# Both transposing transfers of a pair at one place, the last head's first group by TensorE, the last group half a product later

## The chip, the cores and the metric

The kernel runs on one core of one Trainium2 chip. The metric is the device time of one execution in microseconds (us), less is better; several runs are told by their median. Engines are named as the profile names them: PE is TensorE (matmul; PEld its weight loads), DVE is VectorE, ACT is ScalarE, POOL is GpSimd, SP is SyncE. SP computes nothing here; it issues transfers, one after the other, and a transfer whose data aren't ready holds up those behind it in SP's order. POOL issues a few transfers of its own.

## The reference

A decoder trunk of two layers on x of 1 x 1024 x 1024 in float32. Layer 0 is dilated attention: 8 heads of width 128, each in three groups (window, dilation) = (128, 1), (512, 4), (2048, 16); rotary positions on q and k; the three groups of a head are merged by their softmax denominators. Layer 1 is a gated linear attention. After each mixer stands a squared-ReLU MLP; each sub-layer is normalized ahead and added to x. What the change touches is layer 0's attention up to its output product:

```python
qkv = (h @ w_in).reshape(B, S, N_GROUPS, 3, ATTN_HEADS, HEAD_DIM)
for g, (window, dil) in enumerate(DILATED_GROUPS):
    q = apply_rope(qkv[:, :, g, 0], cos, sin) * (HEAD_DIM ** -0.5)
    k = apply_rope(qkv[:, :, g, 1], cos, sin)
    v = qkv[:, :, g, 2].astype(jnp.float32)
    o_g, lse_g = dilated_group_attention(q, k, v, dil, window // dil)
    outs.append(o_g); lses.append(lse_g)
alpha = jax.nn.softmax(jnp.stack(lses, axis=0), axis=0)
o = jnp.sum(alpha[..., None] * jnp.stack(outs, axis=0), axis=0)
return o.reshape(B, S, ATTN_WIDTH).astype(h.dtype) @ w_out
```

## The kernel before, in words

float32 products are made of three matmuls of split operands (`...h` is the high part, `...l` the low one). The attention of layer 0 runs as 24 rounds p = 3 h + g, one for each head h and group g. `Heads.run_head` gives a round 14 half products of 12 matmuls or fewer, in the slots 0, 1, 3, 2, 6, 4, 5; they make q and k of round p (banks `pX`, `pY`, `pV`, `pZ`). `advance()` after each half product moves a clock by one step, and whatever is entered in the agenda for that step (`at(step, function, rank)`) is written into the program there, by rank. So the order of every engine is fixed by the numbers in those calls; with c = 14 p, "c + 3" is the third step of round p.

Of round p itself come: copies of banks by ACT (`e`, L1166), `column` (DVE adds `c`, L1129; SP swaps its halves by two transfers into `cw`, L1130 and L1131; a few steps later DVE multiplies with the rotary tables, L1138 and L1139, and adds into `qT` or `kT`, L1141 or L1146), the loading of raw weights for the next round (`load`, L1121) and their splitting by ACT and DVE (L536, L537).

Entwined with round p, `follow(p - 1, ...)` does the attention of the round before, in four pairs j of query blocks: `scores` (PE, `pS`, L989), `soft` (DVE and ACT, L1003 and L1005, into `pt`), a transposition of `pt`, and `values` (PE, `pO`, L1069; then ACT copies `orow`, L1073, and SP stores it to `og`, L1076 to L1082). The transposition has two forms. `turn` lets PE transpose (`pP`, L1016), and ACT copies the result (L1018). For groups 0 and 2 it goes by memory instead: `halves` (ACT separates the 16-bit halves, L1035; POOL writes them to `pscr`, L1037) and `flip` (SP reads them back by a transposing transfer, `pt<-pscr`, L1048). Pair 0 of group 0 has two such transfers, since its blocks have unequal numbers of keys. `POINTS` holds the steps for scores, turn, values and flip of the four pairs, counted from the round in which the attention is followed; steps of 14 and more fall in the round after it. Attention of group 0 is followed in rounds with p mod 3 = 1, and its flips fall in p mod 3 = 2; those of group 2 fall in p mod 3 = 1.

In rounds p mod 3 = 1 the merge of the head before is entered (`plan_merges`): SP loads `rows` (L1209) in the round p mod 3 = 2, DVE makes minima, differences and shares (`mz`, `md`, `me`, L1216 to L1225), ACT scales by them (L1229), DVE adds (`om`, L1233).

In the last round (p=23) four raw pieces of the output weights (`W.dma`, L136) and the first half of the merged heads 0 to 3 (`ol`, `ahead_h8`, L1294) are loaded, and PE transposes `ol` (`pT`, L260). `tail` then follows the last group beside the output product (`pd`, L214 to L216).

Of the kernel before, what the change touches and what calls it, by code (L numbers as in the profile page):

```python
# [20 lines left out]
P = 128  # L21
# [4 lines left out]
HEADS = 8  # L26
# [16 lines left out]
def hybrid_trunk(ctx, tc, x, norm_mix, norm_mlp, norm_fin, a_in, a_out, g_in, g_up, g_b, g_nw,  # L43
                 g_out, m_up, m_down, tab, msk, gmask, ident_d, out):
    nc = tc.nc
    pe, act, dve, pool, sp = nc.tensor, nc.scalar, nc.vector, nc.gpsimd, nc.sync
# [7 lines left out]
    def h8(shape, dt, name):  # L54
        return wk.tile(shape, dt, name=name, tag="h8", bufs=12)

    def k4(shape, dt, name):
        return wk.tile(shape, dt, name=name, tag="k4", bufs=25)

    def t2(shape, dt, name):  # L60
        return wk.tile(shape, dt, name=name, tag="t2", bufs=8)
# [50 lines left out]
    class Weights:  # L112
# [14 lines left out]
            self.slots.append(src)  # L127
            self.by.append(by)

        def dma(self, by=None):  # L130
            n = self.ndma
            if n < len(self.slots):
                self.ndma += 1
                src = self.slots[n]
                self.raws[n] = k4([P] + list(src.shape[1:]), F32, "raw")
                (by or sp).dma_start(self.raws[n], src)  # L136

        def prep(self, eng=dve):
            n = self.nprep
# [41 lines left out]
    W = Weights()  # L181
# [8 lines left out]
    def add_rows(w, k0, by=None):  # L190
        for k in range(2):
            W.add(w[P * (k0 + k):P * (k0 + k + 1), :], by and by(k0 + k))
# [93 lines left out]
    class Split:  # L286
# [4 lines left out]
        @staticmethod  # L291
        def at(tiles, k):
            n = 4 // len(tiles)
            return tiles[k // n][:, k % n, :]
# [442 lines left out]
    oscr = drp.tile([S, D], F32, name="oscr")  # L737
# [209 lines left out]
    def advance():  # L947
        clock[0] += 1
        for _, fn in sorted(agenda.pop(clock[0], []), key=lambda e: e[0]):
            fn()  # L950
# [9 lines left out]
    def load_values(g, h):  # L960

        v = k4([P, NB, HD], F32, "v")
        c = slice(HD * h, HD * h + HD)
        if g == 0:
            sp.dma_start(v, vscr.rearrange("(b p) g c -> p b g c", p=P)[:, :, 0, c])
        elif g == 1:
            for b in range(2):
                sp.dma_start(v.rearrange("p (r b) c -> p r b c", b=2)[:, :, b, :],
                             vscr[512 * b:512 * b + 512].rearrange("(p r) g c -> p r g c", r=4)[:, :, 1, c])
        else:  # L970
            sp.dma_start(v, vscr.rearrange("(p r) g c -> p r g c", r=8)[:, :, 2, c])
        return v
# [6 lines left out]
    class Attention:  # L979
# [102 lines left out]
                    sp.dma_start(to.rearrange("(p r) c -> p r c", r=8)[:, 2 * j - 2:2 * j + 2, :], row)  # L1082

        def plan(self, c, points, turn, values, flip=None):
            self.by_dma = flip is not None and self.g in (0, 2)
            if flip is not None and not self.by_dma:
                turn, values = (12, 12, 16, 16), (16, 16, 18, 18)

            def get():
                self.v = load_values(self.g, self.h)  # L1090
            at(c + points[0] - 2, get)
            for j in range(4):
                t = c + points[j]
                at(t, lambda j=j: self.scores(j), 2)
                at(t + 1 + (j % 2 and points[j] == points[j - 1]), lambda j=j: self.soft(j), 2)
                if self.by_dma:
                    at(c + turn[j], lambda j=j: self.halves(j), 3)
                    at(c + flip[j], lambda j=j: self.flip(j), 3)
                else:
                    at(c + turn[j], lambda j=j: self.turn(j), 3)  # L1100
                at(c + values[j], lambda j=j: self.values(j), 4)

    class Heads(Up):
# [54 lines left out]
        def plan(self, p):  # L1158
            c = 14 * p
            st = self.st.setdefault(p, {})  # L1160
            self.behind = True

            def keep(b, name):
                def fn():
                    e = t2([P, 512], F32, name)
                    act.activation(e, st[b], AF.Copy)  # L1166
                    st[name] = e
                return fn
            at(c + 3, keep("X", "e1"), 0)
            at(c + 5, lambda: self.column(p, 0, 0, st["Y"], st["e1"]), 1)  # L1170
            at(c + 7, keep("V", "e5"), 0)
            at(c + 9, keep("X", "e2"), 0)
            at(c + 11, lambda: self.column(p, 1, 0, st["V"], st["e2"]), 1)
            at(c + 13, keep("X", "e3"), 0)
            at(c + 13, lambda: self.column(p, 1, 1, st["X"], st["e5"]), 1)
            at(c + 15, lambda: self.column(p, 0, 1, st["Z"], st["e3"]), 1)
            if p == 0:
                for s, t in ((4, 1), (6, 3), (5, 5)):
                    at(c + t, lambda s=s: self.stage(p, s), 7)
            at(c + 1, lambda: self.load(p + 1))  # L1180
            for s, t in ((0, 8), (1, 9), (2, 10), (3, 11), (4, 14), (6, 15), (5, 17)):
                at(c + t, lambda s=s: self.stage(p + 1, s), 7)

        def run_head(self, p):
            self.plan(p)
            if p:
                self.follow(p - 1, 14 * p, self.POINTS if p < self.count - 1 else self.SINGLE)
            for s in self.SLOTS:
# [1 line left out]
                    self.product(p, s, range(2 * half, 2 * half + 2))  # L1190
                    advance()

        POINTS = (8, 8, 12, 12), (11, 12, 15, 16), (21, 21, 25, 25), (14, 15, 18, 19)
        SINGLE = (8, 10, 12, 14), (12, 14, 16, 18), (14, 16, 18, 20)

        def follow(self, p, c, points):
# [91 lines left out]
                reached.add((0, half))  # L1288
            at(clock[0] + 7, last)

    def ahead_h8(pairs, by=sp):

        t = h8([P, 4, 512], F32, "ol")
        by.dma_start(t, oscr[512 * pairs:512 * pairs + 512, 0:512].rearrange("(b p) c -> p b c", p=P))  # L1294
        return [t[:, 0:2, :], t[:, 2:4, :]]

    def ahead_k4(p):
# [4 lines left out]
    def plan_merges(h, c):  # L1302

        rows, part = {}, {}

        def load(half):
            rows[half] = merge_load(h, half)

        def weigh(half):
            part[half] = merge_weights(rows[half])  # L1310

        def join(half):
            del part[half]
            merged(h, half, merge_join(rows.pop(half), dve))
        for half in range(2):
            t = c + 14 + 11 * half
            at(t, lambda half=half: load(half))
            if half and h == HEADS - 2:
                t += 8
            at(t + 4, lambda half=half: weigh(half), 9)  # L1320
            at(t + 5, lambda half=half: merge_shares(rows[half], *part[half]), 9)
            for n in range(4):
                at(t + 6 + n, lambda half=half, n=n: merge_scale(rows[half], part[half][1], n), 9)
            at(t + 10, lambda half=half: join(half), 9)
# [383 lines left out]
    for i, n in enumerate(plan[:-5]):  # L1708
# [5 lines left out]
        if n == vals.STEPS - 2:  # L1714
            heads = Heads(vals.h)
# [38 lines left out]
    ol = []  # L1754
    turned = Turned(ol, x[0])
    for p in range(heads.count):
        h, g = divmod(p, NG)
        if g == 1 and h:
            plan_merges(h - 1, 14 * p)
        if p == heads.count - 1:  # L1760
            for k in range(0, KT, 2):
                add_rows(a_out, k)
            c = 14 * p
            at(c + 1, lambda: (W.dma(pool), W.dma(pool)), 0)
            at(c + 2, lambda: (W.dma(pool), W.dma(pool)), 0)
            at(c + 3, lambda: ol.extend(ahead_h8(0, pool)), 0)
            for t in (5, 6, 7, 8):
                at(c + t, lambda: W.prep(dve), 7)
            at(c + 8, lambda: turned.turn(0), 7)
            at(c + 9, lambda: (turned.load_x(0), turned.load_x(1)))  # L1770
            at(c + 11, lambda: turned.turn(1), 7)
            at(c + 17, lambda: ol.extend(ahead_h8(1)), 9)
        heads.run_head(p)
# [7 lines left out]
    def tail():  # L1781

        c = clock[0]
        heads.follow(heads.count - 1, c, ((6, 7, 8, 9), (9, 10, 11, 12), (11, 12, 13, 14)))
        load, start, finish = merges(HEADS - 1, merged)
        rows = {}
        advance()

        def early(half):
            t = rows[half] = h8([P, 4, 512], F32, "ol2")  # L1790
            sp.dma_start(t[:, :, 0:384], oscr[512 * half:512 * half + 512, 512:896].rearrange("(b p) c -> p b c", p=P))
        at(c + 7, lambda: early(0))
        at(c + 16, lambda: early(1))
        for i, (half, h) in enumerate(((0, 4), (0, 5), (0, 6), (1, 4), (1, 5), (1, 6))):
            at(c + (13 + 3 * i if half == 0 else 21 + i), lambda half=half, h=h: t_head(h, half, rows[half][:, :, HD * (h - 4):HD * (h - 4) + HD]))
        at(c + 15, lambda: (load(0), load(1)), 9)
        at(c + 18, lambda: start(0))
        at(c + 19, lambda: finish(0))
        at(c + 20, lambda: start(1))
        at(c + 21, lambda: finish(1))  # L1800
        steps.extend([advance] * 42)

    tail()


# [587 lines left out]
    ol, turn1 = [], []  # L2393
# [81 lines left out]
```

## Time and profile before

| what | value |
|---|---|
| median of three runs | 2601.3 us (2597.0, 2601.3, 2602.2) |
| profiled execution | 2598.51 us |
| its span, first to last instruction | 2596.7 us |
| mean granted clock of TensorE | 0.998 |
| PE busy | 2574.3 us (99%) |
| DVE, ACT, POOL busy | 72%, 50%, 2% |
| stage of the 24 rounds | from about 246 to 855 us of the span |

The page gives busy times by engine, groups of instructions and transfers. The answers of the trace quoted below are of three kinds: timelines (start, length, engine, line, operation, what it writes and reads, count; in brackets the idle time of the engine ahead of it and what ended it), waits (who waited for what: total, times, longest) and windows (for each engine the busy time in a stretch and the number of instructions, then the granted clock, the busy share of the DMA engines and GB/s).

### The profile page before, as it was taken

The page shows a single profiled execution, that of the slowest core. Times are in us where ns is not written, and L with a number is a line of the kernel's source. Part 1 is how long each engine was busy: PE and PEld are TensorE (multiplying, and loading weights), DVE is VectorE, ACT ScalarE, POOL GpSimd, SP SyncE. Part 2 cuts the span into 40 slices and gives each one's busy share as a digit, 9 for nine tenths or more (in the row PEclk, how much of TensorE's full clock was granted, in tenths as well). Part 3 has the DMA queues.
Part 4 walks back from the last instruction along what each step waited for, and adds up shares of the span by engine and source line. Part 5 has one row for each costly group of instructions (what it writes and reads, how often), then busy time and mean ns, then how long its engine had stood idle before and what let it go on. Part 6 is the DMA issues. An engine that isn't in the chain of part 4 may idle for free.

```text
span 2596.7 us, 33212 instructions
## 1 busy us (share of the span) xinstructions
PE 2574.3 (99%) x11985; PEld 2142.2 (82%) x11985; DVE 1864.0 (72%) x3018; ACT 1298.7 (50%) x2360; POOL 51.8 (2%) x81
## 2 busy tenths in 40 slices
PE   9999999999998999999999999999999999999998
PEld 7888888888887888888888888888888888888887
DVE  7745888888887768666657587887657866656567
ACT  6423455656655446555534345654326554553334
POOL 0000000000001000000000000000000000000000
PEclk9999999999999999999999999999999999999999
DMA  5543677777778633554775452463513544396543
GB/s 183 170 141 115 153 179 200 176 201 196 196 205 221 208 122 127 170 168 139 278 260 182 140 195 96 133 200 98 195 65 118 170 157 155 130 356 203 183 149 131
DMA packets 377911, 445.70 MB, mean 172 GB/s; under 512 B 68145, under 2 KB 240561, under 8 KB 377746
## 3 DMA queue, kind: packets, MB, share of 16 engines
q1 hardware_dynamic: 372850, 428.63, 53.5%
q0 software_dynamic: 4752, 14.68, 1.7%
q8 instruction: 94, 1.54, 0.2%
q14 instruction: 71, 0.58, 0.1%
q10 hardware_dynamic: 144, 0.26, 0.0%
HBM read 279.19 MB, written 127.60 MB: 157 GB/s over the span
## 4 chain that ended last, share of the span: by engine, by line
PE 65%; DVE 3%; ACT 1%; DMA 1%; issue 1%; SPq 0%; DVEq 0%; ACTq 0%
PE pB L1938 13%; PE pX L599 10%; PE pA L1938 10%; PE pV L599 7%; PE pY L599 3%; PE pZ L599 3%; PE pd L216 3%; PE pd L214 3%; PE pd L215 3%; PE pB L830 3%; PE pA L830 2%; PE pT L335 1%; DMA cw<-c 1%; PE pO L2236 1%; PE pU L2218 0%
## 5 line engine op out<-in xcount | busy, mean ns | idle before, releaser
L1938 PE MATMUL pB<-dh 128*128 128x512 f32 x512 | 199.4, 389 | 0.0
L1938 PE MATMUL pB<-dh,dl 128*128 128x512 f32 x512 | 199.2, 389 | 0.0
L1938 PE MATMUL pB<-dl,dh 128*128 128x512 f32 x512 | 199.2, 389 | 0.0
L223 DVE TENSOR_TENSOR dl<-sin,dh 128x1024 fp32r<-128x1024 f32 x112 | 136.8, 1221 | 42.4 <-ACT dh L220 41.8
L220 ACT ACTIVATE dh<-sin 128x1024 fp32r<-128x1024 f32 x112 | 117.8, 1052 | 88.4 <-PE pB L1938 33.4
L220 ACT ACTIVATE dh<-kept 128x1024 fp32r<-128x1024 f32 x64 | 67.9, 1061 | 183.3 <-DVE kept L1903 138.1
L599 PE MATMUL pV<-s4h,wd 128*128 128x512 f32 x448 | 150.3, 397 | 0.0
L1938 PE MATMUL pA<-dl,dh 128*128 128x512 f32 x384 | 149.4, 389 | 0.0
L1938 PE MATMUL pA<-dh,dl 128*128 128x512 f32 x384 | 149.4, 389 | 0.0
L1938 PE MATMUL pA<-dh 128*128 128x512 f32 x384 | 149.4, 389 | 0.0
L1005 ACT ACTIVATE pt<-pt,orow 128x128 f32<-128x128 f32 (+1 forms) x192 | 84.7, 443 | 75.7 <-DVE orow L1003 74.4
L1938 PEld LDWEIGHTS pB<-dh 128*128 128x128 f32 x512 | 96.2, 188 | 19.9
L1938 PEld LDWEIGHTS pB<-dl,dh 128*128 128x128 f32 x512 | 96.2, 188 | 19.9
L1938 PEld LDWEIGHTS pB<-dh,dl 128*128 128x128 f32 x512 | 96.1, 188 | 19.8
L537 DVE TENSOR_TENSOR wal<-raw,wah 128x512 fp32r<-128x512 f32 x112 | 76.2, 687 | 40.8 <-ACT wah L536 40.8
L537 DVE TENSOR_TENSOR wbl<-t,wbh 128x1024 fp32r<-128x1024 f32 x56 | 68.6, 1225 | 43.9 <-ACT wbh L536 43.8
L599 PEld LDWEIGHTS pV<-s4h,wd 128*128 128x128 f32 x448 | 84.2, 188 | 19.3 <-ACT e L1166 1.7
L608 ACT ACTIVATE c<-c 128x512 f32<-128x512 f32 x64 | 40.4, 631 | 118.6 <-DVE c L636 77.5
L223 DVE TENSOR_TENSOR dl<-kept,dh 128x1024 fp32r<-128x1024 f32 x64 | 78.4, 1225 | 24.7 <-ACT dh L220 18.7
L599 PE MATMUL pX<-s3h,wgh 128*128 128x512 f32 x224 | 89.3, 399 | 2.4 <-ACT e L1166 2.4
L599 PE MATMUL pZ<-a22h,wgh 128*128 128x512 f32 x224 | 90.1, 402 | 0.0
L599 PE MATMUL pX<-s2h,wbh 128*128 128x512 f32 x224 | 89.0, 397 | 0.0
(400 smaller groups left out, 7378.7 us busy)
## 6 DMA issues: line engine op xcount, KB each, us to landing
sin<-acts SPq DMA_DIRECT2D x112, 512.0 KB, 3.9
raw<-in_mlp_w_up_dram SPq DMA_DIRECT2D x64, 512.0 KB, 6.0
acts<-s SPq DMA_DIRECT2D x64, 512.0 KB, 3.5
raw<-in_mlp_w_down_dram SPq DMA_DIRECT2D x64, 512.0 KB, 4.8
raw<-in_attn_w_in_dram SPq DMA_DIRECT2D x98, 256.0 KB, 4.7
cw<-c SPq DMA_DIRECT2D x192, 128.0 KB, 2.8
acts<-c SPq DMA_DIRECT2D x64, 256.0 KB, 2.2
kept<-in_mlp_w_down_dram SPq DMA_DIRECT2D x32, 512.0 KB, 5.8
```

Of the source, the lines that this page charges most:

```text
L214: pe.matmul(ps, sh, mh, start=start, stop=False)
L215: pe.matmul(ps, sh, ml, start=False, stop=False)
L216: pe.matmul(ps, sl, mh, start=False, stop=stop)
L220: act.activation(hi, src, AF.Copy)
L223: dve.tensor_tensor(lo, src, hi.bitcast(F32), op=OP.subtract)
L335: pe.transpose(ps[:, k, 128 * i:128 * i + 128], xn[i][:, c:c + 128], ident)
L537: self.remain(lambda: dve.tensor_tensor(lo, src, hi.bitcast(F32), op=OP.subtract))
L599: pe.matmul(st[b], u[:, k, :], v, start=first and k + n == 0, stop=k == 3 and n == 2, skip_group_check=True)
L608: act.activation(r, r, AF.Relu)
L830: pe.matmul(self.acc[s][t], a[:, c], b[:, k, :], start=fresh and m + k + v == 0, stop=m == 1 and k == 1 and v == 2, skip_group_check=True)
L1005: act.activation(pt[:, i, :128 * n], pt[:, i, :128 * n], AF.Exp, scale=-1.0, bias=m, accum_out=self.row[:, r, HD:HD + 1])
L1938: pe.matmul(self.acc[s][t], a[:, k, c], b[:, k, :], start=fresh and m + k + v == 0, stop=m == 7 and k == 1 and v == 2, skip_group_check=True)
```

## The change

Five things, all in layer 0's attention:

1. `plan`: the last head (h = 7) doesn't transpose group 0 by memory any more; PE does, at the steps that group 1 has. Its group 2 was done by PE already.
2. The raw output weights and the first `ol` of the last round are issued by SP, not by POOL, at the same steps.
3. Raw weights of the next round are loaded at c + 3, not c + 1.
4. The flips stand at steps 14, 14, 18, 18, not 14, 15, 18, 19.
5. In the tail, all steps of the last group are one later.

```diff
-        def dma(self, by=None):
+        def dma(self):
...
-                (by or sp).dma_start(self.raws[n], src)
+                sp.dma_start(self.raws[n], src)
...
         def plan(self, c, points, turn, values, flip=None):
-            self.by_dma = flip is not None and self.g in (0, 2)
+            self.by_dma = flip is not None and self.g in (0, 2) and self.h < HEADS - 1
             if flip is not None and not self.by_dma:
                 turn, values = (12, 12, 16, 16), (16, 16, 18, 18)
...
-            at(c + 1, lambda: self.load(p + 1))
+            at(c + 3, lambda: self.load(p + 1))
...
-        POINTS = (8, 8, 12, 12), (11, 12, 15, 16), (21, 21, 25, 25), (14, 15, 18, 19)
+        POINTS = (8, 8, 12, 12), (11, 12, 15, 16), (21, 21, 25, 25), (14, 14, 18, 18)
...
-    def ahead_h8(pairs, by=sp):
+    def ahead_h8(pairs):
...
-        by.dma_start(t, oscr[512 * pairs:512 * pairs + 512, 0:512].rearrange("(b p) c -> p b c", p=P))
+        sp.dma_start(t, oscr[512 * pairs:512 * pairs + 512, 0:512].rearrange("(b p) c -> p b c", p=P))
...
-            at(c + 1, lambda: (W.dma(pool), W.dma(pool)), 0)
-            at(c + 2, lambda: (W.dma(pool), W.dma(pool)), 0)
-            at(c + 3, lambda: ol.extend(ahead_h8(0, pool)), 0)
+            at(c + 1, lambda: (W.dma(), W.dma()), 0)
+            at(c + 2, lambda: (W.dma(), W.dma()), 0)
+            at(c + 3, lambda: ol.extend(ahead_h8(0)), 0)
...
-        heads.follow(heads.count - 1, c, ((6, 7, 8, 9), (9, 10, 11, 12), (11, 12, 13, 14)))
+        heads.follow(heads.count - 1, c, ((7, 8, 9, 10), (10, 11, 12, 13), (12, 13, 14, 15)))
```

SP's order in the rounds p mod 3 = 2 (here p=5), `-` before and `+` now:

```order
+L1048 DMA_TRANSPOSE pt<-pscr_93 128x2x512
 L1209 DMA rows<-og_70 128x4x390
 L1130 DMA cw<-c 64x512
 L1131 DMA cw<-c 64x512
-L1048 DMA_TRANSPOSE pt<-pscr_93 128x2x512
 L1121 DMA raw<-in_attn_w_in_dram 128x4x128 x4
 L1048 DMA_TRANSPOSE pt<-pscr_94 128x2x512
-L1130 DMA cw<-c 64x512
-L1131 DMA cw<-c 64x512
 L1048 DMA_TRANSPOSE pt<-pscr_95 128x2x512
+L1130 DMA cw<-c 64x512
+L1131 DMA cw<-c 64x512
```

The second pair's transfer now stands ahead of the merge's `rows` and of a pair of `cw`, and the fourth pair's ahead of the next pair of `cw`; the raw weights keep their place behind the first `cw`.

SP's order in the last round (p=23), before:

```order
L1048 DMA_TRANSPOSE pt<-pscr_92 128x1x256
L1048 DMA_TRANSPOSE pt<-pscr_92 128x2x256
L1209 DMA rows<-og_76 128x4x390
L1130 DMA cw<-c 64x512
L1131 DMA cw<-c 64x512
L1048 DMA_TRANSPOSE pt<-pscr_93 128x2x512
L1048 DMA_TRANSPOSE pt<-pscr_94 128x2x512
L1130 DMA cw<-c 64x512
L1131 DMA cw<-c 64x512
L1048 DMA_TRANSPOSE pt<-pscr_95 128x2x512
L968 DMA v<-vscr 128x4x128 x2
```

and now:

```order
L1209 DMA rows<-og_76 128x4x390
L136 DMA raw<-in_attn_w_out_dram 128x1024 x2
L1130 DMA cw<-c 64x512
L1131 DMA cw<-c 64x512
L136 DMA raw<-in_attn_w_out_dram 128x1024 x2
L1076 DMA og_77<-orow 128x4x130
L1294 DMA ol<-oscr 128x4x512
L1076 DMA og_77<-orow 128x4x130
L1130 DMA cw<-c 64x512
L1131 DMA cw<-c 64x512
L968 DMA v<-vscr 128x4x128 x2
```

The five transposing transfers are gone; weights and `ol` stand among the small ones, and the stores `og` of group 0, which followed `v` before, come ahead of the second `cw`.

PE's order in the tail, at the first scores of the last group, `-` before and `+` now:

```order
 L215 MATMUL pd<-wlo,oTh 128x512
 L216 MATMUL pd<-whi,oTl 128x512
-L989 MATMUL pS<-kT,qT 128x128 x2
 L1069 MATMUL pO<-v,pt 128x128 x3
 L989 MATMUL pS<-kT,qT 128x128 x2
```

The first scores of the last group stand behind the last `pO` of the group before; the second scores move behind the twelve matmuls that follow.

## The prediction

> **What bounds the kernel now.** I read the page first, then the waits of TensorE over the stage that the change touches, then the timelines of the places where those waits sit.
>
> ```profile
> PE 2574.3 (99%) x11985; PEld 2142.2 (82%) x11985; DVE 1864.0 (72%) x3018; ACT 1298.7 (50%) x2360; POOL 51.8 (2%) x81
> ```
>
> TensorE (PE) is busy for 99% of the span, so an edit can gain only what is left of its idle time, or time lost at a lower clock. The list of waits from 246 to 866 us (the 24 rounds of layer 0's attention and the start of its tail) shows how little that is. Columns: total us, times, longest.
>
> ```profile
> PE pO L1069 <- DMA pt<-pscr: 7.0, 5, 5.4
> PE pX L599 <- ACT e L1166: 2.4, 7, 1.1
> PE pS L989 <- DVE qT L1146: 2.2, 3, 1.7
> ...
> PEld pV L599 <- ACT e L1166: 1.7, 6, 0.4
> ```
>
> Five waits for a transposing transfer (`pt<-pscr`) make 7.0 us, one of them alone 5.4. That one stands in the last round (p=23):
>
> ```profile
> 826.17 0.39 PE L599 MATMUL pX<-s2h,wbl 128*128 128x512 f32 x1
> 826.40 0.83 PE L1069 MATMUL pO<-v,pt 128*128 128x128 f32 x6
> 832.63 2.07 PE L1069 MATMUL pO<-v,pt 128*128 128x128 f32 x8 [5.41 <-DMA pt<-pscr]
> ...
> 835.36 0.63 PE L599 MATMUL pX<-s2h,wbl 128*128 128x512 f32 x1
> 835.79 0.63 PE L599 MATMUL pX<-s2h,wbh 128*128 128x512 f32 x1
> ...
> 837.07 0.82 PE L989 MATMUL pS<-kT,qT 128*128 128x128 f32 x4
> 837.72 1.04 PE L260 MATMUL pT<-ident,ol 128*128 128x128 f32 x8
> ```
>
> After the wait the matmuls start 0.43 us apart (835.36 to 835.79) instead of 0.23 (826.17 to 826.40): a half clock, until 837.07. From 832.63 to 837.07 that costs half of 4.44, **2.2 us**. The windows' granted clock (the number ahead of the DMA share) says the same, and that the DMA engines are full there:
>
> ```profile
> 820.00:830.00 10.00, 7.22 (x35) 5.91 (x34) 4.80 (x6) 1.59 (x3) 2.10 (x4) 1.00 1.11 306
> 830.00:840.00 10.00, 7.37 (x33) 6.43 (x34) 7.20 (x13) 6.05 (x13) 0.22 (x1) 0.66 1.16 301
> ```
>
> What fills them are the issues of SP and POOL in this round: 780 KB of `rows` (512 x 3 x 130 words), four pieces of 512 KB of raw output weights on POOL's queue and 1 MB of `ol`, while SP's sequencer stands 10.34 us in two transposing transfers and DVE waits 2.89 us for `cw`:
>
> ```profile
> 819.23 0.53 SPq L1209 DMA_DIRECT2D rows<-og  x1
> ...
> 821.12 10.34 SPq L1048 DMA_TRANSPOSE pt<-pscr  x2
> ```
>
> ```profile
> 824.15 0.69 DVE L1138 TENSOR_TENSOR cw<-cw,tab 128x512 f32<-128x512 f32 x1 [2.89 <-DMA cw<-c]
> ```
>
> ```profile
> 814.84 1.15 POOL L136 DMA_DIRECT2D raw<-in_attn_w_out_dram  x2
> ...
> 819.71 1.22 POOL L136 DMA_DIRECT2D raw<-in_attn_w_out_dram  x2
> ...
> 829.42 0.80 POOL L1294 DMA_DIRECT2D ol<-oscr  x1 [7.43 <-issue]
> ```
>
> **The change, part by part.** *Last head's group 0 by TensorE.* Its transfers go, and with them the wait of 5.41 and the slow clock of 2.2: **−7.6**. In their place come 15 transposes. A round that has them shows six:
>
> ```profile
> 764.22 0.82 PE L1016 MATMUL pP<-ident,pt 128*128 128x128 f32 x6
> 764.80 0.48 PE L599 MATMUL pZ<-a22h,wgh 128*128 128x512 f32 x1
> ```
>
> The next matmul starts 0.58 us later, 0.097 each; the matmul after them takes 0.09 longer than its like (0.48 against 0.39). Fifteen in two places: 1.46 + 0.2 = **+1.6**. The rule beside it: the Trainium skill, "TensorE: Matmul & The Clock Gate", section "Part 4: PE-mode transpose", gives about 275 ns for one 128x128 transpose within a kernel. By that figure 15 would be 4.1 us and the whole result 2.5 worse; the trace shows lengths near it (0.82 − 5 × 0.097 = 0.33 for one) but overlapped starts, and the starts set the pace.
>
> *Output weights and `ol` on SP's queue.* They leave POOL's queue and stand in SP's between `rows`, the `cw` transfers and the store `og`. Their bytes with `rows` (0.8 MB), weights (2.1), `ol` (1.05) and the small ones (0.5) make 4.5 MB; at the 306 GB/s of the window that is 14.7 us. From an issue at about 817 `ol` is there at about 832. PE wants it at 837.72 − 7.6 + 0.8 (eight of the transposes) + 1.8 (the second half of `pO`, which moves ahead of it) = 832.7. Estimate **+0.4** for this and for the conversions of weights behind it; bounds 0 and 2 (no wait; `ol` 2 us late). The scores ahead of it want `qT` at 837.07 − 7.6 + 0.8 + 1.8 = 832.1; its `cw` stands behind `rows` and half of the weights (0.8 + 1.05 + 0.25 MB, 6.9 us at 306 GB/s from 819, so about 826), and `qT` follows 2.4 us behind the first product with `cw` (372.08 to 373.41 + 1.11 below), so it is there near 829. I charge nothing; without that cover it is rival 3. The rule beside it: the Trainium skill, "DMA: Bandwidth & Descriptors", section "Queues, rings and completion order", says that each DMA engine takes turns between queue rows by packets and consumes one row in ring order. By it, `cw` no longer takes turns with POOL's weights but waits behind the first megabyte. The rows agree so far as DVE waited long for `cw` with both queues loaded (2.89 us); no run here shows one queue alone.
>
> *Both transposing transfers of a pair at one place.* This touches every round with p mod 3 = 1 or 2; what it does is worked out for p=5. First SP's issues, then what DVE, ACT and PE do with them:
>
> ```profile
> 361.64 2.51 SPq L1048 DMA_TRANSPOSE pt<-pscr  x2
> 364.24 0.53 SPq L1209 DMA_DIRECT2D rows<-og  x1
> 364.88 0.47 SPq L1130 DMA_DIRECT2D cw<-c  x1
> ...
> 366.08 1.83 SPq L1048 DMA_TRANSPOSE pt<-pscr  x1
> ...
> 375.95 1.29 SPq L1048 DMA_TRANSPOSE pt<-pscr  x1
> ```
>
> ```profile
> 372.08 0.69 DVE L1138 TENSOR_TENSOR cw<-cw,tab 128x512 f32<-128x512 f32 x1 [1.02 <-DMA cw<-c]
> ...
> 373.41 1.11 DVE L1146 TENSOR_TENSOR qT<-c,cw 128x512 f32<-128x512 f32 x1
> ```
>
> ```profile
> 375.27 0.98 ACT L1229 ACTIVATE rows<-rows,me 128x128 f32<-128x128 f32 x3 [4.56 <-DVE me L1225]
> 376.16 0.57 ACT L1166 ACTIVATE e<-pV 128x512 f32<-128x512 f32 x1
> ```
>
> ```profile
> 373.01 1.16 PE L1069 MATMUL pO<-v,pt 128*128 128x128 f32 x8 [0.33 <-DMA pt<-pscr]
> ...
> 376.78 0.50 PE L599 MATMUL pV<-s4h,wd 128*128 128x512 f32 x1
> ```
>
> DVE waits for `cw` (until 372.08), builds `qT`, then the shares `me` of the merge; ACT waits for these (4.56 us), scales, and only then copies `e`; PE starts 376.78, which is 376.16 + 0.57 + 0.05. So PE there starts when `cw` lets it, and the row of weight loads that wait for `e` (1.7 us, **6** times) says that it is so in six rounds. The sixth, p=20, has the same 0.05: 754.39 + 0.57 against 755.02, give or take a hundredth.
>
> ```profile
> 750.35 0.69 DVE L1138 TENSOR_TENSOR cw<-cw,tab 128x512 f32<-128x512 f32 x1 [0.61 <-DMA cw<-c]
> ...
> 754.39 0.57 ACT L1166 ACTIVATE e<-pV 128x512 f32<-128x512 f32 x1
> ...
> 755.02 0.50 PE L599 MATMUL pV<-s4h,wd 128*128 128x512 f32 x1
> ```
>
> Two things follow. The small waits for the transposing transfers (7.0 − 5.4 = 1.6 us in four rounds) stand upstream of a bound by `cw`; taking them away gains nothing, PE waits 3 us later instead. And the second transfer, now ahead of `rows` and `cw`, makes these later by δ, which PE pays six times. Bounds of δ: at 0, the transfer slips in beside them. By issue, 1.29 + 0.1 = 1.4 (the row at 375.95 and a gap). By landing, the transfer was there 0.93 after `cw` (373.01 against 372.08); if one queue moves the same bytes in another order, `cw` now takes that later place. If issue and part of the transfer add up (a transposing transfer needs 2.3 us at the least, from issue to landing), 2.2:
>
> ```profile
> DMA to landing us min/median/max: 2.3/3.5/11.5
> ```
>
> I take 1.0, nearest the landings, since the queue is never idle there: 6 × 1.0 = **+6.0** (0 to 13). Cover: none, that is the point. p=2 has no merge in it, and p mod 3 = 1 has neither `rows` nor a bound by `e` in the list of six: nothing for them. The input weights are issued where SP comes to them anyway; their later place (two half products, 2.7 us, in p mod 3 = 0) I charge at nothing, because the only wait of PE that could come from them is not in the list; without that cover some tenths a round.
>
> *The tail.* PE waits 1.74 us for the last `qT`:
>
> ```profile
> 861.49 0.39 PE L216 MATMUL pd<-whi,oTl 128*128 128x512 f32 x1
> 863.61 0.68 PE L989 MATMUL pS<-kT,qT 128*128 128x128 f32 x4 [1.74 <-DVE qT L1146]
> 864.13 0.83 PE L1069 MATMUL pO<-v,pt 128*128 128x128 f32 x6
> ```
>
> One step later puts the first scores behind this `pO` (0.83 long, about 0.6 between starts), not behind the next twelve matmuls; only the second scores go there. So 0.6 of the 1.74 is filled: **−0.6** (bounds 0 and −1.7).
>
> Sum: −7.6 + 1.6 + 0.4 + 6.0 − 0.6 = **−0.2**. The profiled execution took 2598.51 us (span 2596.7); it becomes 2598.3. The median of the runs shown is 2601.3, 2.8 above the profiled one, so I expect a median of **2601**.
>
> **Rivals.** 1) *The six rounds don't pay* (δ = 0: `rows`, `cw` and the transfer share the engines). Then −6.2, or −7.8 if the 1.6 is gained too: 2595.1 to 2593.5. For it: `cw` is only 256 KB, and where transfers share the 16 engines the order of issue need not be the order of landing. Against: the handover from `e` to PE within 0.05 in these rounds, which leaves no room for any δ above 0. 2) *The six rounds pay in full*, slower: place, `cw` behind the second transfer in p = 5, 8, 11, 14, 17, 20; price δ = 2.2, so −6.2 + 13.2 = +7.0: 2608. It decides from δ = 1.9 (−6.2 + 6 × 1.9 = 5.2). For it: the transfer's 1.83 issue at 366.08; against: the 0.93 between landings. 3) *The last round waits anew*: `ol` or `qT` lands behind 2 MB on the one queue, PE idles over 3 us at the first `pT<-ident,ol` and runs at half clock again, as it did after 5.41: 3.3 + 2 more, +5 on the sum: 2606. For it: 8.3 us lay between the issue of `ol` (829.42) and its first transpose (837.72), and now 2 MB stand ahead of it on its own queue; against: it is issued about 8 us earlier. That the change doesn't do what it says I leave out: the transposes stand in the new order of TensorE.
>
> **How the numbers follow.** 0.2% of 2601.3 is 5.2 us, about what a measurement of this kernel tells from no change: "same" is 2596.1 to 2606.5. Chances: forecast 0.50 (its own range 2597 to 2605), rival 1 0.25, rival 2 0.13, rival 3 0.12. Faster: nearly all of rival 1 and a twentieth of the forecast, 0.27. Slower: most of rival 2 and some of rival 3, 0.16. Same: 0.57. The range 2593.5 to 2606.5 leaves out rival 2 and the far end of rival 1.
>
> **What would show it.** Right: no `pO<-DMA` wait near 827, clock 1.00 in the last round, six `cw` waits of DVE about 1 us longer and the starts of `pV<-s4h` still 0.05 behind `e`; the distance between starts of rounds 5 and 6 about 1 us longer; a wait for `qT` of about 1.1 in the tail. Wrong: `cw` waits as before with the round 5 to 20 no longer (rival 1), 2 us longer each (rival 2), a new wait at `pT<-ident,ol` or a clock below 1 near 833 (rival 3).

## The result: slower by 1.1%

| | before | changed |
|---|---|---|
| median of the runs | 2600.7 us (2597.0 to 2602.2) | 2629.2 us (2626.3 to 2631.8) |
| span of the profiled execution | 2596.7 us | 2626.8 us |
| PE busy | 2574.3 us | 2585.8 us |

The ratio is 1.0111, with a 95% interval of 1.0094 to 1.0129. The forecast was 2601, the range ended at 2606.5, and the slower rival at 2608; all are far below the measured time.

Where the time went is read from the starts of the rounds (the first matmul `pX<-a11h` of each in TensorE's timeline). The changed kernel's start minus the one before, in us, each from one profiled execution:

| round | 5 | 6 | 8 | 9 | 11 | 12 | 15 | 18 | 21 | 23 | behind the tail's product |
|---|---|---|---|---|---|---|---|---|---|---|---|
| changed | -0.2 | 5.2 | 4.9 | 7.2 | 7.3 | 15.7 | 21.6 | 27.6 | 34.2 | 34.1 | 28.8 |

The time is lost inside rounds 5, 8, 11, 14, 17 and 20 (5.4, 2.3, 8.4, 6.1, 6.0 and 6.6 us), and 5.3 us are won back in the last round and its tail. The page of the changed kernel and its list of waits (all engines, from 246 to 890 us: the rounds and the start of the tail; total, times, longest):

```profile
span 2626.8 us, 33208 instructions
...
PE 2585.8 (98%) x12000; PEld 2150.5 (82%) x12000; DVE 1863.9 (71%) x3018; ACT 1297.1 (49%) x2359; POOL 45.5 (2%) x71
```

```profile
DVE cw L1138 <- DMA cw<-c: 46.6, 23, 4.0
PE pS L989 <- DVE qT L1146: 24.9, 7, 6.3
DVE mz L1216 <- DMA rows<-og: 21.9, 8, 4.0
PE pV L599 <- ACT e L1166: 1.6, 2, 0.9
```

PE's waits for `pt<-pscr` (7.0 us before) are gone; 24.9 us of waits for `qT` stand in their place. DVE waits 21.9 us for `rows`, 4.0 before within this stretch, and 46.6 for `cw`, 23.6 before. Round 11 shows the chain. Timelines of SP, DVE and PE, and one window:

```profile
525.40 3.85 SPq L1048 DMA_TRANSPOSE pt<-pscr  x3
529.35 0.53 SPq L1209 DMA_DIRECT2D rows<-og  x1
```

```profile
515.28 0.69 DVE L1138 TENSOR_TENSOR cw<-cw,tab 128x512 f32<-128x512 f32 x1 [4.00 <-DMA cw<-c]
...
537.97 0.17 DVE L1216 TENSOR_REDUCE mz<-rows 128x4 f32<-128x12 f32 x1 [4.02 <-DMA rows<-og]
...
540.65 1.07 DVE L1146 TENSOR_TENSOR qT<-c,cw 128x512 f32<-128x512 f32 x1
```

```profile
541.78 2.50 PE L989 MATMUL pS<-kT,qT 128*128 128x256 f32 x6 [6.30 <-DVE qT L1146]
```

```profile
541.70:545.00 3.30, 3.22 (x8) 2.43 (x9) 1.27 (x9) 2.54 (x8) 0.00 (x0) 0.50 0.97 216
```

`rows` is issued behind three transposing transfers and reaches DVE 8.6 us after its issue (529.35 to 537.97). The minimum `mz`, which wants `rows`, stands in DVE's order ahead of the products with `cw`, so `qT` is late, PE idles 6.30 us and then works at half clock (0.50 in the window). Round 5, the first to lose time, shows `mz` before and now:

```profile
370.08 0.17 DVE L1216 TENSOR_REDUCE mz<-rows 128x4 f32<-128x12 f32 x1
```

```profile
374.02 0.17 DVE L1216 TENSOR_REDUCE mz<-rows 128x4 f32<-128x12 f32 x1 [4.04 <-DMA rows<-og]
```

From the issue of `rows` it was 5.8 us at most before (364.24 to 370.08, without a wait) and is 8.6 now (365.39 to 374.02). In round 11 the transfers are also issued late, 3.2 us behind the first matmul of the round (522.16), where the first of them stood 0.7 ahead of it before (514.16 against 514.86): the wait of 4.00 for a `cw`, in round 10, had made DVE late, and with it the `cw` that SP issues ahead of them.

The last round went as it was meant to. PE's timeline there, and the first scores of the tail:

```profile
854.52 1.92 PE L1016 MATMUL pP<-ident,pt 128*128 128x128 f32 x8 [0.63 <-ACT pt L1005]
856.27 1.73 PE L1069 MATMUL pO<-v,pt 128*128 128x128 f32 x14
...
869.46 1.07 PE L260 MATMUL pT<-ident,ol 128*128 128x128 f32 x8 [0.81 <-DMA ol<-oscr]
...
893.15 0.68 PE L989 MATMUL pS<-kT,qT 128*128 128x128 f32 x4 [0.94 <-DVE qT L1146]
```

No wait for a transposing transfer is left there; 0.6 us for `pt` and 0.8 for `ol` stand in its place, and the tail's wait for `qT` is 0.9, where 1.1 was forecast.

### The profile page after: what moved, and what is told of

Its sections match the earlier page's. It is cut to its first block, busy times and chain, and to the rows that moved or that the text cites. A ratio compares the mean times of both kernels' runs of the same rounds, so it can differ in the third digit from the quotient of the medians.

```text
span 2626.8 us, 33208 instructions
## 1 busy us (share of the span) xinstructions
PE 2585.8 (98%) x12000; PEld 2150.5 (82%) x12000; DVE 1863.9 (71%) x3018; ACT 1297.1 (49%) x2359; POOL 45.5 (2%) x71
## 4 chain that ended last, share of the span: by engine, by line
PE 65%; DVE 0%; ACT 0%; issue 0%; ACTq 0%; DVEq 0%
PE pB L1938 13%; PE pX L599 10%; PE pA L1938 10%; PE pV L599 7%; PE pB L830 3%; PE pY L599 3%; PE pZ L599 3%; PE pd L216 3%; PE pd L214 3%; PE pd L215 3%; PE pA L830 2%; PE pT L335 1%; PE pO L2236 1%; PE pU L2218 0%; PE pO L2235 0%; PE pT L260 0%
## 5 line engine op out<-in xcount | busy, mean ns | idle before, releaser
L599 PE MATMUL pV<-s4h,wd 128*128 128x512 f32 x448 | 155.9, 410 | 1.6 <-ACT e L1166 1.6
L989 PE MATMUL pS<-kT,qT 128*128 128x128 f32 (+1 forms) x384 | 75.9, 339 | 25.9 <-DVE qT L1146 25.9
L1138 DVE TENSOR_TENSOR cw<-cw,tab 128x512 f32<-128x512 f32 x96 | 65.9, 687 | 46.9 <-DMA cw<-c 46.6
L989 PEld LDWEIGHTS pS<-kT,qT 128*128 128x128 f32 x384 | 62.2, 199 | 34.8 <-DVE qT L1146 26.5
```

What stands on the lines that cost most here:

```text
L599: pe.matmul(st[b], u[:, k, :], v, start=first and k + n == 0, stop=k == 3 and n == 2, skip_group_check=True)
L989: pe.matmul(ps[:, i, :128 * n], self.qT[:, 128 * b:128 * b + 128], self.kT[:, k0:k0 + 128 * n], start=True, stop=True)
L1138: dve.tensor_tensor(w, w, ctab[:, 1, sl], op=OP.mult)
```

## Experiments

Each kernel is told by its edit against the kernel before or the changed one. A difference is against the median of the kernel before on the same chip in the same runs (2598.8 to 2599.6 us). Starts of rounds and lists of waits come from one profiled execution of each kernel, and that can lie off the median: the one with the second pair's flip moved took 2618.6 (median 2623.3), the same with `rows` first 2596.7 (2600.8).

### Which of the edits cost

**Flips alone**, the kernel before with

```diff
-... (21, 21, 25, 25), (14, 15, 18, 19)
+... (21, 21, 25, 25), (14, 14, 18, 18)
```

> The kernel before with the flips at 14, 14, 18, 18 and nothing else changed. Theory 1 (SP's order alone: a transposing transfer put ahead of rows and of cw makes these late, DVE builds qT late, PE waits and falls to half clock): nearly the whole loss, +25 to +40 us against before (the changed kernel lost 34.1 us up to the start of the last round and won 5.3 back in it), most of it as waits of PE pS for qT in rounds 5, 8, 11, 14, 17, 20. Theory 2 (the later loading of raw weights puts these ahead of a cw and makes DVE late from round to round; the flips cost only what round 5 shows, 5.4 us at the first and 2 to 3 at the others): +8 to +20 us.

Measured 2623.6, ratio 1.0096 (1.0081 to 1.0111): +24.8, just below theory 1's range and above theory 2's. Up to the start of round 23 it lost 18.5 us, which fits theory 2's price for the rounds (5.4 and five times 2 to 3, 15 to 20), and in the last round and the tail 10.0 more, which neither theory named and which the changed kernel, without flips there, doesn't pay.

**Loading alone**, the kernel before with

```diff
-            at(c + 1, lambda: self.load(p + 1))
+            at(c + 3, lambda: self.load(p + 1))
```

> The kernel before with the raw weights of the next round loaded at c + 3 and nothing else changed. Theory 1: within 2 us of before, since the flips alone do it. Theory 2: +10 to +25 us, with waits of DVE for cw in the rounds p mod 3 = 0 that before has not.

Measured 2617.5, ratio 1.0072 (1.0057 to 1.0088): +18.7. Theory 1 falls: loading costs by itself, 14.5 us up to round 23. The two single losses up to there add up to 33, and the changed kernel lost 34.1, so in these profiles they nearly add up.

**Last head alone**, the kernel before with edits 1 and 2 (TensorE for group 0 of the last head, weights and `ol` on SP's queue):

> The kernel before with the last head's group 0 transposed by TensorE, and the output weights and ol on SP's queue; flips, loading and tail as before. Both theories: the six rounds as before, and in the last round the wait of 5.4 and the half clock gone: -5 to -7 us (the changed kernel won 5.3 us there). If the gain there hangs on the other edits, within 2 us of before.

Measured 2592.3, ratio 0.9975 (0.9965 to 0.9985): -6.5, as both theories had it.

**Flips back**, the changed kernel with the flips at 14, 15, 18, 19:

> The changed kernel with the flips back at 14, 15, 18, 19; last head, queue, loading and tail as changed. Theory 1: faster than before by 5 to 7 us, the six waits for qT gone. Theory 2: still slower than before by 5 to 20 us.

Measured 2609.1, ratio 1.0041 (1.0026 to 1.0056): +10.3. Theory 2: without the flips the loading still costs.

### Why the later loading costs

Only the rounds with p mod 3 = 0 get another order by this edit (in the others SP comes to the raw weights at the same place). SP's issues in round 9, with the loading at c + 1:

```profile
470.70 2.24 SPq L1121 DMA_DIRECT2D raw<-in_attn_w_in_dram  x4
474.17 4.36 SPq L1079 DMA_DIRECT2D og<-orow  x4
478.63 0.47 SPq L1130 DMA_DIRECT2D cw<-c  x1
```

and at c + 3, in the kernel with the loading alone:

```profile
474.86 0.88 SPq L1079 DMA_DIRECT2D og<-orow  x2
475.84 2.16 SPq L1121 DMA_DIRECT2D raw<-in_attn_w_in_dram  x4
478.10 1.14 SPq L1079 DMA_DIRECT2D og<-orow  x2
479.34 1.58 SPq L1130 DMA_DIRECT2D cw<-c  x1
```

`cw` now comes 1.3 us behind the issue of 1 MB of weights (475.84 + 2.16 to 479.34, two stores between), where 5.7 us lay between before (470.70 + 2.24 to 478.63). What DVE makes of it, before and with the later loading:

```profile
482.27 0.69 DVE L1138 TENSOR_TENSOR cw<-cw,tab 128x512 f32<-128x512 f32 x1
```

```profile
485.51 0.69 DVE L1138 TENSOR_TENSOR cw<-cw,tab 128x512 f32<-128x512 f32 x1 [2.41 <-DMA cw<-c]
```

DVE starts 3.2 us later, of which PE's round is only 0.8 late, and stays late through round 10. In round 11 the transposing transfers then start late, and PE waits for them, in the list of waits of PE (8.0 of it in the last round, 12.4 in rounds 5 to 20, where before had 1.6) and at that place:

```profile
PE pO L1069 <- DMA pt<-pscr: 20.4, 7, 8.0
```

```profile
528.93 1.80 PE L1069 MATMUL pO<-v,pt 128*128 128x128 f32 x8 [2.99 <-DMA pt<-pscr]
```

**Loading behind `cw`** tells the `cw` from the weights themselves as the cause:

```diff
-            at(c + 1, lambda: self.load(p + 1))
+            at(c + (5 if p % 3 == 0 else 1), lambda: self.load(p + 1))
```

> The kernel before with raw weights of the next round loaded at c + 5 in rounds p mod 3 = 0, behind the stores og and behind that round's cw, and at c + 1 elsewhere. Theory A (at c + 3 the 1 MB ahead of this cw held up DVE, which then started the next two rounds late): that loss (18.7) is gone, 0 to +5. Theory B (the raw weights themselves came too late for ACT's splitting): more than at c + 3, +18 to +35.

Measured 2603.4, ratio 1.0018 (1.0009 to 1.0027): +4.2. Later still, but behind the small transfer, the same weights cost a quarter of it. Theory A holds: what counts is what they hold up, not when they come.

### Why the flips cost

**Second pair's flip alone**, flips at (14, 14, 18, 19):

> The kernel before with only the second pair's flip moved (14, 14, 18, 19): it stands ahead of rows and cw in the rounds p mod 3 = 2, the fourth pair's stays behind the next cw. Theory A (what counts is the transfer ahead of rows, whose landing DVE waits for): +15 to +25 of the 24.8 us that both flips cost, DVE waiting 3 to 4 us for rows in each of six rounds and 10 in the last. Theory B (DVE must also be late from the rounds before, by the fourth pair's flip ahead of cw): +5 to +12.

Measured 2623.3, ratio 1.0096 (1.0081 to 1.0112): +23.7, as theory A had it. The four executions lie far apart (2618.6 to 2629.9).

**Fourth pair's flip alone**, flips at (14, 15, 18, 18):

> The kernel before with only the fourth pair's flip moved (14, 15, 18, 18): it stands ahead of a cw in the rounds p mod 3 = 1 and 2, rows and the second pair's flip as before. Theory A: within 4 us of before, since that cw has slack. Theory B: +5 to +15, as DVE waits longer for that cw and starts the next round late.

Measured 2606.7, ratio 1.0030 (1.0018 to 1.0042): +7.1, in theory B's range: the flip ahead of a `cw` isn't free. But 23.7 and 7.1 make more than the 24.8 of both together, so beside the second pair's flip the fourth's adds little. It also loses its time elsewhere: 7.0 us in rounds 6, 9, 12, 15, 18 and 21, where the changed kernel loses nothing, while rounds 5 to 20 came out 1.2 us shorter.

The starts of the rounds show 2.6, 2.3, 3.3, 1.8, 3.3 and 5.6 us lost with the second pair's flip in rounds 5 to 20 (18.9) and 4.3 in the last round. By windows over these six rounds PE is idle for 15.9 us (2.9 before) and busy for 164.7 (158.8 before): 13.0 of the 18.9 is waiting, 5.9 slower work.

**A plain transfer in that place** asks whether bytes do it or the transposition. Ahead of `rows` in rounds 5 to 20, the kernel before with

```diff
+            if not half and h < HEADS - 2:
+                sp.dma_start(spare[h], a_in[0:128, 0:512])
             rows[half] = merge_load(h, half)
```

> The kernel before with one more plain transfer of 256 KB (input weights to a spare place in memory that nothing reads) issued by SP just ahead of rows in rounds 5, 8, 11, 14, 17 and 20: the bytes of the second pair's transposing transfer, in its place, without transposition. Theory A (a transposing transfer holds up what is queued behind it for its whole length, while the DMA engines stand half empty; plain bytes cost only their own 0.9 us at 300 GB/s): cw lands 0.5 to 1.2 us later, +3 to +8 us. Theory B (any 256 KB ahead of rows costs this): +14 to +20 us, as the second pair's flip does in these six rounds (16).

Measured 2603.2, ratio 1.0014 (1.0005 to 1.0023): +3.9. By the starts of the rounds the six lost 5.4 us, against 18.9 for as many transposing bytes. That is theory A's price; PE's waits are another kind, 0.8 to 1.1 us for `pt<-pscr` in each of the six.

**`rows` ahead of the flips**, first with the second pair's flip moved:

```diff
-            at(t, lambda half=half: load(half))
+            at(t, lambda half=half: load(half), 5 if half else 2)
```

> The kernel with only the second pair's flip moved (14, 14, 18, 19), and rows issued ahead of all flips of the round, so that SP's order is rows, flips of pairs 0 and 1, cw. Theory A (the transposing transfers delay what stands behind them, here cw): DVE waits for cw instead of rows and the loss stays, +12 to +22. Theory B (only the landing of rows counted): +0 to +6, waits for rows gone.

Measured 2600.8, ratio 1.0005 (0.9996 to 1.0014): +1.5, no change that can be told. Theory B: with `rows` out of the way the loss of 23.7 shrinks to what can't be told from none, though `cw` still stands behind the flip. My theory A was too broad. (The flip isn't free even so: from round 5 to round 23 this kernel's profile, the fastest of its ten, won 1.5 us, the one below with `rows` first and the flips in their old places 3.8.) The windows of round 5 say why; behind the instructions' busy times stand granted clock, DMA share and GB/s. Before, with the second pair's flip moved, with the plain transfer, and with the second pair's flip moved and `rows` first, in this order:

```profile
363.50:366.00 2.50, 2.50 (x13) 2.07 (x12) 2.46 (x4) 2.00 (x3) 0.82 (x2) 1.00 0.52 81
366.00:368.50 2.50, 2.50 (x13) 2.07 (x12) 2.46 (x5) 1.55 (x2) 0.62 (x1) 1.00 0.84 205
```

```profile
363.50:366.00 2.50, 2.50 (x13) 2.07 (x12) 2.47 (x4) 1.79 (x4) 1.34 (x2) 1.00 0.50 114
366.00:368.50 2.50, 2.50 (x13) 2.07 (x12) 2.47 (x5) 1.23 (x2) 0.11 (x1) 1.00 0.95 233
```

```profile
363.50:366.00 2.50, 2.50 (x12) 2.07 (x12) 2.46 (x4) 1.77 (x3) 1.40 (x2) 1.00 0.55 98
366.00:368.50 2.50, 2.50 (x12) 2.07 (x12) 2.46 (x5) 1.20 (x2) 0.04 (x1) 1.00 1.03 372
```

```profile
363.50:366.00 2.50, 2.50 (x13) 2.07 (x12) 2.47 (x5) 1.78 (x4) 1.45 (x2) 1.00 1.14 362
366.00:368.50 2.50, 2.50 (x13) 2.07 (x12) 2.47 (x5) 1.04 (x2) 0.00 (x0) 1.00 1.18 200
```

While transposing transfers stand at the head of the queue, the DMA engines are half empty (0.50 to 0.55, 81 to 114 GB/s), and what is queued behind waits. With `rows` ahead, its bytes fill the same stretch (1.14, 362 GB/s). In the second stretch 233 GB/s follow the moved flip, little more than before (205), and 372 the plain bytes.

What waits for what is seen in the packets. `rows` moves in packets of 512 bytes to 2 KB, a transposing transfer in packets under 512. The first line holds the 2 us behind the issue of `rows` (365.11) in the kernel with the second pair's flip moved, the second 2 us of the same with `rows` first, where the transposing transfers are issued from 362.04 on:

```profile
DMA packets 1000, 0.50 MB, mean 249 GB/s; under 512 B 936, under 2 KB 936, under 8 KB 1000
```

```profile
DMA packets 426, 0.66 MB, mean 331 GB/s; under 512 B 2, under 2 KB 426, under 8 KB 426
```

In the first no packet of `rows` moves while the third transposing transfer runs (365.10 to 367.36, 256 KB in 2.3 us); in the second the transposing ones move none while `rows` does (the 2 small packets are 4 bytes each). The raw weights, which now follow `rows` more closely on SP, aren't the cause: their first packet starts at 371.38, when nine tenths of `rows` have moved. A part of the delay is SP's own: it issues `rows` 4.0 us behind the first transposing transfer of the round (361.11 to 365.11), 2.6 before (361.64 to 364.24) and 3.2 with the plain one (361.05 to 364.29).

### Versions that beat both

**Last head, queue and tail**, without the flips and the loading:

> The kernel before with the last head's group 0 by TensorE, weights and ol on SP's queue and the tail one step later; flips and loading of raw weights as before. If the two edits of SP's order in the 24 rounds carry the whole loss, this is the last-head kernel (2592.3) with the tail's part: -6.5 to -8 us against before, of which the tail 0 to 1. If the tail is worth what it waited (1.7), -8 to -9.

Measured 2592.2, ratio 0.9972 (0.9963 to 0.9982): -7.4. Beside the last head alone (2592.3) the tail brings nothing that can be told.

**Weights left on POOL's queue**, edit 1 alone:

> The kernel before with the last head's group 0 by TensorE, weights and ol still issued by POOL. Theory A (the wait of 5.4 came from the transposing transfers alone): -6 to -8 us, as with the queue changed. Theory B (POOL's 3 MB beside SP's small transfers hold cw up): within 3 us of before, DVE still waiting near 3 us for cw in the last round.

Measured 2594.7, ratio 0.9984 (0.9975 to 0.9994): -4.8, between the theories. The interval overlaps that of the kernel with the queue changed too, so most of the gain is the transposing transfers' own, and whether the queue adds 2 us stays open. DVE's wait for `cw` in the last round, 2.89 before, is 1.15 here and gone with the queue changed.

**`rows` first on top of the best**, with the edit of rank shown above:

> The best kernel so far (last head by TensorE, queue, tail; 2592.2) with rows issued ahead of the first flips in rounds p mod 3 = 2. If rows and then cw land earlier by the two short transfers (2.5 us of issue), DVE's wait of 0.5 to 1.1 for cw in these rounds is gone and PE's wait for e with it, 0 to 3 us faster than the best. If cw stays behind the flips or PE waits for pt in its place, within 1 us of it, or 2 slower.

Measured 2586.5, ratio 0.9951 (0.9939 to 0.9964): -12.7, the fastest of all, 5.7 under the best so far where 0 to 3 were expected. SP and DVE in round 5:

```profile
361.90 0.37 SPq L1209 DMA_DIRECT2D rows<-og  x1
362.38 2.41 SPq L1048 DMA_TRANSPOSE pt<-pscr  x2
```

```profile
369.76 0.17 DVE L1216 TENSOR_REDUCE mz<-rows 128x4 f32<-128x12 f32 x1
...
370.66 0.68 DVE L1138 TENSOR_TENSOR cw<-cw,tab 128x512 f32<-128x512 f32 x1
```

DVE waits for neither; the product with `cw` starts at 370.66 instead of 372.08.

### The two causes in the changed kernel itself

The changed kernel with `rows` first, and the same with the loading back at c + 1:

> The changed kernel with one edit: rows issued ahead of the flips in rounds p mod 3 = 2. Theory A (of its loss up to the last round, 34 us, the part of the flips is that rows stands behind them; the rest is the later loading): 18 to 22 us of it go, which leaves 2606 to 2613. Theory B (flips and loading hold each other up, so that rows alone frees little): 2618 or more.

> The changed kernel with two edits: rows ahead of the flips and the loading back at c + 1. It differs from the kernel with rows first (2586.5) only by the flips at one place. Theory A (with rows ahead, the flips at one place cost little): 2586 to 2593. Theory B (the second and fourth pair's transfers hold up cw as well): 2595 to 2605.

Measured 2616.8, ratio 1.0065 (1.0048 to 1.0082), and 2592.9, ratio 0.9981 (0.9971 to 0.9991). The second lies at the end of theory A's range, the first between its theories: of 34.3 us lost from round 5 to round 23, `rows` first takes back 9.7, not 18 to 22. With the later loading the lateness of `cw` goes on; the list of waits for that kernel (all engines, 246 to 900 us):

```profile
PE pO L1069 <- DMA pt<-pscr: 12.0, 9, 2.0
...
DVE cw L1138 <- DMA cw<-c: 66.4, 27, 4.2
...
DVE mz L1216 <- DMA rows<-og: 0.6, 1, 0.6
```

The wait for `rows` is gone (0.6), that for `cw` is 66.4, more than in the changed kernel. So with late weights the flips ahead of `cw` do cost, by about 10 us (24.7 lost from round 5 to round 23, 15.0 with the loading alone). With the loading back the kernel is faster than before, and some 6 us slower than with the flips at their old places (2586.5, from other runs): the edit that named the change gains nothing even where its harm is taken away.

## Why the prediction was wrong, point by point

- **The rounds were right, the path and the size were not.** The prediction said that in six rounds PE hangs on `cw`, that the second pair's transfer makes `rows` and `cw` late, and that PE pays it six times, with nothing gained from the small waits. The six rounds did pay, and the small waits gained nothing. But the wait that decides is that for `rows`, which got no row and no term. DVE's `mz` stands ahead of the products with `cw`, so in round 5 DVE waits 4.04 us for `rows` and then 0.15 for `cw`, and PE waits for `qT` at `pS`, not only for `e` at `pV`, the handover that I watched. With `rows` out of the way DVE waits 1.37 for `cw` behind three transposing transfers, 1.02 before, and the loss is gone: for `cw` alone δ was not too small.
- **The term that failed is δ = 1.0.** With that flip alone PE lost 18.9 us in six rounds, some 3.1 in each (6.0 were forecast for all). I had it from the distance between the landings of `cw` and of the transfer, 0.93, with the reason that one queue moves the same bytes in another order. The runs show that the order changes the rate: ahead of `rows` the transposing transfers hold the queue at 81 to 114 GB/s, the third alone for 2.3 us. PE's waiting alone, 13.0 us or 2.2 a round, comes to the upper bound that I had from issue and transfer together; what lies above it is half clock, for which δ had no place.
- **A step was priced at nothing that cost 18.7 us.** For the later loading I looked at who reads the weights, found no wait of PE on them, and charged nothing, or some tenths a round. What I didn't name is what is queued behind them on SP: `cw` of the same round. The loading behind `cw` (+4.2) shows it.
- **The fourth pair's flip** got no term; it costs 7.1 us alone, and 1.1 beside the second's.
- **Half clock.** I counted it where it would vanish and not where it would come. By windows over the six rounds PE is idle for 26.7 us (2.9 before) and busy for 169.8 (158.8 before): of the 34.8 us that they became longer 23.7 is waiting and 11.0 slower work, by the half clock in five of them (the windows below).
- **The last round was right in sum, with luck in its terms.** -7.6 + 1.6 + 0.4 - 0.6 = -6.2 was forecast from its start to the end of the tail; -5.3 is measured in the changed kernel and -7.5 with the last head alone, without the tail's part (-8.2 less the -0.6 that it had at the start of round 23). The wait for `ol` is 0.8 (0.4 forecast). Eight transposes took 1.75 us up to the next start (854.52 to 856.27), where I had 0.8 at 0.097 each, and 0.63 of waiting stood ahead of them. The row had come from transposes whose input was ready; here the list of waits from 853 to 858 us shows their weight loads waiting for the last `pt` of ACT:

```profile
PEld pP L1016 <- ACT pt L1005: 1.9, 4, 1.0
```

- **The tail.** The wait shrank from 1.74 to 0.94, as forecast, but no gain in time can be told.
- **The rivals.** The slower one named place and mechanism and priced it at +7. The ranges of both δ and the loading ended where my reasons did, not where the rows left the question open.

The Trainium skill, "DMA: Bandwidth & Descriptors", section "Queues, rings and completion order", says that each engine consumes the descriptors of one row in ring order. The trace agrees in round 5: no packet of `rows` moves in the 2 us behind its issue, while the transposing transfer ahead runs, and with `rows` ahead it is the other way round. That rule stood in the prediction for the weights of the last round, where it did little; it belonged to rounds 5 to 20.

## What to carry to other kernels

When a transfer is moved on an issuing queue, list what stands behind it at its new place, and price that, not the moved transfer's own reader. A transposing transfer at the head of a queue can hold it for longer than its bytes (2.3 us for 256 KB here), so put the large plain load that someone waits for ahead of it. If a schedule has six equal rounds with no slack, a microsecond there is six, and several with the half clock that follows.

## What the runs showed of the hardware that was not expected

**A transposing transfer holds up what is queued behind it for longer than as many plain bytes do.** 256 KB of plain bytes ahead of `rows` cost 5.4 us in six rounds, 256 KB transposing 18.9; with `rows` ahead of the latter the rounds lost nothing against before. The plain transfer also had larger packets (2 KB) and went to memory, not into `pt`; which of the three differences counts wasn't tried.

**Half clock comes in whole stretches of 3.41 us, and where a wait falls decides.** The granted clock in the changed kernel, in rounds 5, 11, 14, 17 and 20, where it fell, and in round 8, where it didn't:

```profile
378.69:385.52 6.83, 6.13 (x15) 4.45 (x14) 4.59 (x12) 6.83 (x23) 0.00 (x0) 0.50 0.69 180
539.12:545.95 6.83, 4.17 (x11) 3.19 (x12) 4.18 (x12) 3.49 (x10) 0.00 (x0) 0.50 1.09 222
621.04:627.87 6.83, 4.54 (x12) 3.47 (x13) 4.26 (x13) 3.85 (x12) 0.00 (x0) 0.50 1.11 222
702.96:709.79 6.83, 5.39 (x14) 4.10 (x15) 4.00 (x13) 4.70 (x14) 0.00 (x0) 0.50 1.07 247
784.88:791.71 6.83, 5.87 (x15) 4.49 (x16) 4.11 (x12) 5.18 (x16) 0.00 (x0) 0.50 1.10 249
```

```profile
457.70:461.00 3.30, 2.44 (x11) 1.81 (x12) 1.20 (x8) 2.60 (x8) 0.00 (x0) 1.00 1.02 188
```

Each stretch is 6.83 us long, twice 3.41, and their starts lie 160.43, 81.92, 81.92 and 81.92 apart, 47 and 24 times 3.41. In the kernel with the second pair's flip moved a wait of 1.98 didn't bring it, and a shorter one of 1.84 did:

```profile
376.64 1.35 PE L989 MATMUL pS<-kT,qT 128*128 128x256 f32 x6 [1.98 <-DVE qT L1146]
...
532.50 2.14 PE L989 MATMUL pS<-kT,qT 128*128 128x256 f32 x6 [1.84 <-DVE qT L1146]
```

```profile
376.60:380.00 3.40, 2.51 (x11) 1.87 (x12) 1.50 (x9) 2.67 (x8) 0.00 (x0) 1.00 1.10 217
...
532.90:536.30 3.40, 3.33 (x10) 2.24 (x9) 1.56 (x8) 3.11 (x9) 0.00 (x0) 0.50 1.05 218
```

The starts divide the time of an execution into windows of 3.41 us. PE's idle time was summed by window from 250 to 880 us, in the kernel before, the changed one and those with the flips, the loading or the second pair's flip alone. It is 1.84 us or more in each window at whose end the clock fell, and 1.74 or less in each at whose end it stayed full. The wait of 1.98 is cut in two by the end of a window, that of 1.84 isn't. So in the changed kernel round 5, with 2.35 us idle in one window, lost 5.4 us, and round 8, with 1.37 at most, 2.3. The Trainium skill, "TensorE: Matmul & The Clock Gate", section "Part 1: The HAM clock gate (the "warmup" mystery)", tells of an activity window of about 3.4 us that runs freely, and puts the half clock behind an idle one. The traces agree on the window, by the distances of the starts, but not on the idle one: 1.84 us idle in a window was enough here.

**A small step in layer 1.** All eight kernels with the last head by TensorE show a wait of PE for DVE (`dl`, L815) of 0.76 or 0.77 us far from any edit, at 1653.63 in the changed one; the eight others don't. The changed kernel and the one with last head, queue and tail lose 1.2 to 1.3 us there. Its cause stays open.
